# The last rotary score product on 128 rows of the array in place of 64

## The chip, the core and the metric

The kernel runs on one core of one Trainium2 chip. The metric is the device time of one execution in microseconds (us). Three runs of the kernel before gave 1396.41, 1398.60 and 1401.24 us; their median is 1398.6 us. TensorE (PE in the rows) multiplies matrices; VectorE (DVE), ScalarE (ACT) and GpSimd (POOL) do the rest, and nearly all transfers are issued from the queue of SyncE (SP).

## The reference, cut to what matters

One layer of a hybrid block on 1024 tokens: an input projection, a gated delta rule, latent attention with a rotary part, an output projection with a norm, a gated MLP, and a last norm. The change lies in the attention. Its four heads share one rotary key of 64 features, and its scores are

```python
s = jnp.einsum("bqhd,bkhd->bhqk", qn, k_nope) + jnp.einsum("bqhd,bkd->bhqk", qr, k_rope)
q_chunk = (blk * Q_BLOCK + jnp.arange(Q_BLOCK)) // CHUNK
allowed = key_chunk[None, :] <= q_chunk[:, None]
s = jnp.where(allowed, s.astype(jnp.float32) * scale, -jnp.inf)
pr = jax.nn.softmax(s, axis=-1).astype(v.dtype)
return jnp.einsum("bhqk,bkhd->bqhd", pr, v)
```

with 128 features without rotation (qn, k_nope) and 64 with it (qr, k_rope), and queries in 8 blocks of 128.

## The kernel before

**Numbers in two parts.** TensorE multiplies operands of type float32r. To keep float32 accuracy a value is split into a high part, rounded to float32r, and a low part, the rest. A product of two such values is then three products: high by high, low by high and high by low.

**A block of scores.** `score(h, qb)` (line 1146) makes the scores of head h and query block qb: 128 queries against the (qb + 1) * 128 keys that they may see, in one or two pieces b of at most 512 keys. Each piece is a sum of five matmuls into one bank: three for the features without rotation (`qnh` by `knh`, `qnh` by `knl`, `qnl` by `knh`), and two for the rotary ones. For these a tile `q_rot[h][hf]` has the high parts of the 64 rotary query features in rows 0 to 63 and the low parts in rows 64 to 127, and a tile `k_hh[b]` has the high parts of the keys twice, in the lower and the upper 64 rows. So the fourth matmul, `q_rot` by `k_hh` on 128 rows, does high by high and low by high at once. The fifth does high by low: it takes rows 0 to 63 of `q_rot` against `k_ll[b]`, the low parts of the keys, a tile of 64 rows. There are 32 blocks and 48 pieces, so 48 matmuls of each of the five kinds.

**What uses the scores.** `softmax` puts the mask into the block (a memset on VectorE), takes the maximum on VectorE, the exponential on ScalarE, and scales on VectorE. `transposed` turns the probabilities on TensorE (tiles `pt`), splits them (`pth` on ScalarE, `ptl` on VectorE), and `attended` multiplies them with the values (tiles `ov`). In round n the loop at line 1263 does the scores of pair n of query blocks between the transposes and products of pair n - 2. Scores lie in two banks of kind A, so a block waits for the exponential of the block before the last. In the rounds of the last head VectorE and ScalarE also split the weights of the output projection (tiles `wo`).

**Where the rotary keys come from.** `split_keys` (line 965) runs for both halves hf of the keys, while the last input projections (tiles `cq`) are on TensorE: ScalarE casts the high part, GpSimd subtracts for the low part, and SyncE's queue copies the high part to the upper rows of `k_hh`. The rotary queries are rotated later on VectorE and GpSimd (`rotate_queries`), written to `rot_d` in device memory and read back as `q_rot`.

**What sets the order.** A planner of coroutines with rough times decides at build time in which order the instructions are written: `wait(tile)` gives the time until a tile is ready by the planner's own clock, and a coroutine that yields goes on that much later. Every engine then runs its instructions in the written order, and SyncE's queue issues its transfers in order too, each one behind the waits of those ahead.

Of the kernel before, what the change touches and what calls it, by code (L numbers as in the profile page):

```python
# [17 lines left out]
P = 128  # L18
# [52 lines left out]
def hybrid_block_kernel(  # L71
# [22 lines left out]
    def SR(name, shape=None):  # L94
        return S(name, shape, F32R)
# [8 lines left out]
    # Coroutines yield the time until they go on; the clock is the tensor engine's. Rough times of the  # L104
    # instructions tell when a tile is ready.
# [32 lines left out]
    def settle(*aps):  # L138
        """Lets the others go on until the tiles are ready."""
        while events and wait(*aps) > 0.0 and events[0][0] < clock[0] + wait(*aps):  # L140
            hop()
# [5 lines left out]
    def book(engine, cost, delay, outs, ins):  # L147
        """The time at which an instruction ends."""
        near = delay if engine == "pe" else 0.0
        at = max([clock[0], busy.get(engine, 0.0)]  # L150
                 + [ready.get(k, 0.0) - (near if writer.get(k) is engine else 0.0) for k in outs + ins])
        busy[engine] = at + cost
        for k in outs:
            ready[k], writer[k] = at + cost + delay, engine
        for k in outs + ins:
            used[k] = max(used.get(k, 0.0), at + cost + delay)
        return at + cost

    class Engine:
        """An engine whose instructions are booked, and go out in the order in which they are written if pinned."""  # L160
# [49 lines left out]
    def room(*tags):  # L210
        """The time until a bank of each kind can be had."""
        return max(0.0, max(used.get(banks[t][0], 0.0) for t in tags) - clock[0])
# [30 lines left out]
    def split_w(src, shape, name, sub=None):  # L243
        """DMA a weight block and split it into two float32r parts whose sum is the block."""
# [6 lines left out]
    def prepare(w, src, shape, name, tags=("raw", "whi", "wlo")):  # L251
        """split_w, spread over the time it takes."""
# [9 lines left out]
    def mm3(outs, nk, w_hi, w_lo, r_hi, r_lo, order=((0,), (1,), (2,))):  # L262
        """outs[i] = sum_k w(k)^T r(k, i): three float32r products per block."""
# [8 lines left out]
    def rsqrt(y, v, n, e=None):  # L272
        """y = v^-0.5 on [P, n]: a bit-level first guess and Newton steps."""
        e = e or dve
        a = T(f"rs_a{n}", n)
# [7 lines left out]
    def inverse_root(y, h, e=None, between=()):  # L283
        """y = (2 h)^-0.5 on [P, 1], as rsqrt; other work fills the pauses."""
# [25 lines left out]
    # The first tokens come by halves of the features, so that the first products start early.  # L310
# [70 lines left out]
    # The tensor engine's clock doubles after some microseconds of work.  # L381
# [141 lines left out]
    def conv_half(f, y, ps, hf, then):  # L523
        """One half of a causal convolution of width 4 and its SiLU."""
# [14 lines left out]
    # Keys stay as they are: with r = 1 / |k|, the normed rule is that of k with the strength beta r^2  # L539
    # and the values v / r, so that only per-token factors change.  # L540
# [31 lines left out]
    def decays():  # L572
        """exp(G_i - G_j) of the running sums of the log decays, 0 above the diagonal."""
# [89 lines left out]
    def inverse(j):  # L663
        """The L of two chunks becomes ((I + L)^-1)^T, by 32 -> 64 -> 128 block elimination."""
# [55 lines left out]
    def chunk(t):  # L720
        """What chunk t needs besides the state: the attention inside it, its query norms and values."""
# [23 lines left out]
    def step(t):  # L745
        """The new values of chunk t and the state after it."""
# [34 lines left out]
    def chunk_out(t, qc, et, vn, state):  # L781
        """The outputs of chunk t, normed, gated and feature-major."""
# [85 lines left out]
    # The queries stay without the factor of their norm, which the softmax applies with its scale.  # L868
# [19 lines left out]
    def token_factors(name, rs, n):  # L888
        """1 / the root mean square over the n features, [token, block]."""
# [60 lines left out]
    def rotate_keys():  # L950
        """In place."""
# [13 lines left out]
    def split_keys():  # L965
        for hf in range(2):
            hh, ll = SR(f"k_hh{hf}"), SR(f"k_ll{hf}", [64, 512])
            split(hh[0:64], ll, krr[hf], pool)
            yield wait(hh)
            sync.dma_start(out=f32(hh[64:128]), in_=f32(hh[0:64]))  # L970
            k_hh.append(hh)
            k_ll.append(ll)
            yield 2.0
# [172 lines left out]
    def score(h, qb):  # L1146
        """Starts the probabilities of a query block, [query, key]."""
# [5 lines left out]
        for b in range((nk + 511) // 512):  # L1153
# [6 lines left out]
            mm(o_, q_rot[h][hf][0:64, qs], k_ll[b][:, 0:n], start=False)  # L1160
# [5 lines left out]
    def transposed(h, qq, j2):  # L1166
        """The probabilities of two query blocks for two key blocks, [key, query], split; 0 above the diagonal."""
# [29 lines left out]
    def attend(h, qq):  # L1197
        """Yields where a block of scores fits in."""
# [15 lines left out]
    def split_wide(name, src, tag):  # L1214
        """A [P, 2, 512] block as two pairs of float32r parts."""
# [19 lines left out]
    # The delta rule's part of the output projection of the first tokens fills in where attention leaves room.  # L1235
# [74 lines left out]
    def row_factors(st, n, e=None):  # L1310
        """The means of the rows and what gives 1 / deviation."""
# [9 lines left out]
    def layer_norm(r, g, b, e=None, last=None):  # L1321
        """r [P, 2, 512], over its whole rows, in place."""
# [19 lines left out]
    def transpose_h(hf, k2):  # L1342
        """Two of the blocks of h^T."""
# [12 lines left out]
    # The blocks of h^T (features of the lower and upper half, tokens of the first and second) and their sums  # L1356
    # T1 = B12 - B11, T2 = B22 - T1, T3 = B22 - B12, -T4 = B21 - T2, as pairs of parts.
# [3 lines left out]
    def add_up(hf, k, x):  # L1361
        """What block k of h^T, x, gives to the sums."""
# [90 lines left out]
    # The gates, by halves q of the columns, in Winograd's form of Strassen's product as explained below: A = w^T in  # L1453
    # blocks of column halves and halves of the inner sum, B = h^T.
# [51 lines left out]
    def gate_rows(q, i, j, c):  # L1506
        """Column quarter 2 q + i of the rows of half j gets its gated embedding; c: the sums with the bias."""
# [40 lines left out]
    def embed_rows(n, t):  # L1548
        """The projected embeddings of a row block."""
# [32 lines left out]
    g_d = [tc.dram_tile([P, 1024], F32, name=f"g{f}_d") for f in range(NFT)]  # L1582

    # u^T = w^T h^T for a feature of the gate and its partner, by Winograd's form of Strassen's product: with
    # A = w^T in 2 x 2 blocks (gate and partner, halves of the inner sum), S1 = A21 + A22, S2 = S1 - A11,
    # S3 = A11 - A21, S4 = A12 - S2 and P1 = A11 B11, P2 = A12 B21, P3 = S4 B22, P4 = A22 T4, P5 = S1 T1,
    # P6 = S2 T2, P7 = S3 T3 it is C11 = P1 + P2, C12 = P1 + P6 + P5 + P3, C21 = P1 + P6 + P7 - P4,
    # C22 = P1 + P6 + P7 + P5. Sums of products stay in PSUM where they can.
    ffn = [{} for _ in range(NFT)]

    def operand(f, i):
        """The left operand of product i of feature block f."""
# [41 lines left out]
    def conv(f, n, y, src):  # L1634
        """y = the convolution of src, a half of the tokens."""
# [5 lines left out]
    def conv_edge(f, n, y, before):  # L1641
        """What the tokens before it give to the second half."""
# [48 lines left out]
    # out = g w for pairs of feature blocks in the same form: A = g in blocks of token halves and the two features,  # L1691
    # B = w in blocks of the two features and column halves.
# [41 lines left out]
    def prepare_down(n):  # L1734
        """The operands of a step, and sums for later ones; gives out the vector engine's work."""
# [35 lines left out]
    # The features left over, in the plain way: gT[f][half] and wd[f][half] as pairs of parts.  # L1771
# [17 lines left out]
    def down_last(gT, wd, g, b):  # L1789
        """The last features; every row block is normed and goes out as soon as it is complete."""  # L1790
# [8 lines left out]
        def sum_factors(r, sums, e):  # L1799
            """row_factors from the sums of the halves of the rows."""  # L1800
# [160 lines left out]
```

## Time and profile before

| | |
|---|---|
| median of three runs | 1398.6 us |
| lowest, highest | 1396.41, 1401.24 us |
| span of the profiled execution | 1395.9 us |
| busy in the span: PE, DVE, ACT, POOL | 1354.1, 985.0, 626.6, 189.5 us |
| attention's stretch | from about 402 to 545 us of the span |
| mean granted clock of TensorE | 0.988 of full speed |

The span runs from the first to the last instruction of one profiled execution; the profile gives no other time of that execution. The median of the runs is 2.7 us above it. A matmul's duration in the rows includes its way through the array and overlaps with the next one's; what a matmul takes from the stream is the distance between its start and the next start.

### The profile page before, as it was taken

The page shows a single profiled execution, that of the slowest core. Times are in us where ns is not written, and L with a number is a line of the kernel's source. Part 1 is how long each engine was busy: PE and PEld are TensorE (multiplying, and loading weights), DVE is VectorE, ACT ScalarE, POOL GpSimd, SP SyncE. Part 2 cuts the span into 40 slices and gives each one's busy share as a digit, 9 for nine tenths or more (in the row PEclk, how much of TensorE's full clock was granted, in tenths as well). Part 3 has the DMA queues.
Part 4 walks back from the last instruction along what each step waited for, and adds up shares of the span by engine and source line. Part 5 has one row for each costly group of instructions (what it writes and reads, how often), then busy time and mean ns, then how long its engine had stood idle before and what let it go on. Part 6 is the DMA issues. An engine that isn't in the chain of part 4 may idle for free.

```text
span 1395.9 us, 19833 instructions
## 1 busy us (share of the span) xinstructions
PE 1354.1 (97%) x7185; PEld 1127.2 (81%) x7185; DVE 985.0 (71%) x1781; ACT 626.6 (45%) x1213; POOL 189.5 (14%) x418
## 2 busy tenths in 40 slices
PE   9999997999989999999999999999999999999995
PEld 6788885888867877888998888888888888888884
DVE  3646233365366675776989888888888887998857
ACT  3444223555434454135535555555555555444511
POOL 0231540034430000221000000000000000000026
PEclk9999998999999999999999999999999999999998
DMA  7035434434431224335552222222222239505112
GB/s 215 30 114 163 122 111 99 142 100 147 119 112 42 84 65 142 91 108 166 190 182 65 91 91 88 78 83 69 91 91 91 76 127 386 173 9 205 53 41 102
DMA packets 180929, 158.93 MB, mean 114 GB/s; under 512 B 26106, under 2 KB 140640, under 8 KB 180832
## 3 DMA queue, kind: packets, MB, share of 16 engines
q1 hardware_dynamic: 180624, 157.41, 36.3%
q8 instruction: 56, 0.92, 0.3%
q14 instruction: 41, 0.34, 0.1%
q10 hardware_dynamic: 144, 0.26, 0.1%
q0 software_dynamic: 64, 0.00, 0.0%
HBM read 117.53 MB, written 39.85 MB: 113 GB/s over the span
## 4 chain that ended last, share of the span: by engine, by line
PE 65%; DVE 4%; POOL 2%; ACT 2%; issue 2%; DMA 1%; SPq 0%; DVEq 0%; ACTq 0%; POOLq 0%
PE ffX L198 17%; PE ffZ L198 9%; PE dX L198 7%; PE dP L198 5%; PE ffY L198 4%; PE s L198 4%; PE mixp L198 4%; PE gX L198 3%; PE ov L198 2%; PE cq L198 2%; PE gY0P L198 1%; PE gY1P L198 1%; POOL rs_u L169 1%; PE pt L201 1%; DVE h L169 1%
## 5 line engine op out<-in xcount | busy, mean ns | idle before, releaser
L169 POOL TENSOR_SCALAR ln_v<-ln_ss 128x1 f32<-128x1 f32 x7 | 9.0, 1285 | 710.6 <-ACT sink L169 710.1
L198 PE MATMUL dX<-dP,dP 128*128 128x512 f32 x432 | 99.5, 389 | 0.0
L198 PEld LDWEIGHTS dX<-dP,dP 128*128 128x128 f32 x432 | 81.0, 188 | 17.1 <-DVE h L169 0.2
L169 DVE SCALAR_TENSOR_TENSOR gate<-c,vec,gate 128x511 f32<-128x511 f32 (+1 forms) x132 | 69.9, 571 | 11.4 <-ACT gate L169 10.6
L198 PE MATMUL dP<-dP,dP 128*128 128x512 f32 x324 | 75.4, 390 | 0.0
L198 PEld LDWEIGHTS dP<-dP,dP 128*128 128x128 f32 x324 | 60.6, 188 | 13.3 <-DVE h L169 0.9
L169 ACT CAST dP<-b 128x512 fp32r<-128x512 f32 x45 | 28.0, 622 | 59.6 <-issue 20.8
L169 ACT COPY c<-ffX 128x512 f32<-128x512 f32 x44 | 25.8, 586 | 38.9 <-PE ffX L198 38.9
L169 ACT ACTIVATE gate<-c,vec 128x512 f32<-128x512 f32 x44 | 35.9, 816 | 14.7 <-DVE c L169 12.6
L169 DVE SCALAR_TENSOR_TENSOR u<-ffX,vec,u 128x511 f32<-128x511 f32 (+1 forms) x88 | 40.2, 478 | 0.1
L169 ACT ACTIVATE p<-s,mx,q_f 128x128 f32<-128x128 f32 (+7 forms) x32 | 26.7, 835 | 28.6 <-DVE mx L169 26.7
L169 DVE SCALAR_TENSOR_TENSOR u<-c,vec,u 128x511 f32<-128x511 f32 (+1 forms) x44 | 33.0, 751 | 7.3 <-ACT u L169 6.6
L169 DVE TENSOR_TENSOR dP<-b,dP 128x512 fp32r<-128x512 f32 x45 | 31.1, 691 | 8.5 <-ACT dP L169 7.0
L169 ACT ACTIVATE gate<-gate 128x512 f32<-128x512 f32 x44 | 27.6, 627 | 12.2 <-DVE gate L169 12.2
L198 PE MATMUL ov<-pth,v 128*128 128x256 f32 x160 | 33.0, 299 | 0.1
L169 DVE TENSOR_TENSOR ptl<-pt,pth 128x512 fp32r<-128x512 f32 (+1 forms) x40 | 24.8, 633 | 11.1 <-ACT pth L169 10.6
L169 DVE TENSOR_TENSOR dP<-a,dP 128x512 fp32r<-128x512 f32 x45 | 31.0, 689 | 0.0
L169 DVE TENSOR_TENSOR u<-u,gate 128x512 f32<-128x512 f32 x44 | 30.1, 685 | 0.0
L169 ACT CAST dP<-a 128x512 fp32r<-128x512 f32 x45 | 27.7, 616 | 5.1 <-issue 2.2
L169 DVE SCALAR_TENSOR_TENSOR kt<-k,vec,kt 128x512 f32<-128x512 f32 (+3 forms) x24 | 16.4, 742 | 19.0 <-ACT kt L169 19.0
L169 POOL TENSOR_TENSOR h<-h,b 128x1024 f32<-128x1024 f32 x8 | 19.3, 2415 | 76.4 <-DVE h L169 75.1
L198 PEld LDWEIGHTS ov<-pth,v 128*128 128x128 f32 x160 | 24.8, 189 | 4.4 <-issue 1.8
(1373 smaller groups left out, 4181.1 us busy)
## 6 DMA issues: line engine op xcount, KB each, us to landing
wup<-in_ffn_w_up_dram SPq DMA_DIRECT2D x88, 256.0 KB
b<-in_ffn_w_down_dram SPq DMA_DIRECT2D x54, 256.0 KB
a<-g_d SPq DMA_DIRECT2D x45, 256.0 KB
g_d<-u SPq DMA_DIRECT2D x44, 256.0 KB
wgP_raw<-in_ple_w_gate_dram SPq DMA_DIRECT2D x16, 512.0 KB
wo_raw<-in_w_out_dram SPq DMA_DIRECT2D x8, 512.0 KB
xres<-in_x_dram SPq DMA_DIRECT2D x8, 512.0 KB
pp_d<-pp SPq DMA_DIRECT2D x16, 256.0 KB
```

The costliest lines, as they stand in the source:

```text
L169: ins = f(*a, **k)
L198: on_pe(nc.tensor.matmul(o, a, b, start=start, stop=stop, **k_), max((k - 1.0) * a.shape[-1] / 1900.0, n * k / 2370.0), o, a, b)
L201: on_pe(nc.tensor.transpose(o, a, i), 0.107, o, a)
```

## The change

The tiles `k_ll` get 128 rows. Their lower 64 rows are computed as before, and a new transfer on SyncE's queue copies them to the upper 64; for that `split_keys` also waits for `k_ll` in the planner's time. The fifth matmul takes all 128 rows of `q_rot`. It then also adds low by low. The diff also takes out comments, which are left out here.

```diff
     def split_keys():
         for hf in range(2):
-            hh, ll = SR(f"k_hh{hf}"), SR(f"k_ll{hf}", [64, 512])
-            split(hh[0:64], ll, krr[hf], pool)
+            hh, ll = SR(f"k_hh{hf}"), SR(f"k_ll{hf}")
+            split(hh[0:64], ll[0:64], krr[hf], pool)
             yield wait(hh)
             sync.dma_start(out=f32(hh[64:128]), in_=f32(hh[0:64]))
+            yield wait(ll)
+            sync.dma_start(out=f32(ll[64:128]), in_=f32(ll[0:64]))
             k_hh.append(hh)
             k_ll.append(ll)
             yield 2.0
...
             mm(o_, q_rot[h][hf][:, qs], k_hh[b][:, 0:n], start=False, stop=False)
-            mm(o_, q_rot[h][hf][0:64, qs], k_ll[b][:, 0:n], start=False)
+            mm(o_, q_rot[h][hf][:, qs], k_ll[b][:, 0:n], start=False)
             go()
```

On TensorE, VectorE and GpSimd the order of the instructions is the same. It differs on SyncE's queue and on ScalarE, in the last stretch of the input projections. On SyncE's queue, where the rotary keys are copied and weights for the attention are fetched (`wqr`, `wqn`, `wkn`), it is before

```order
L169 DMA wqr_raw<-in_mla_w_q_up_dram 128x4x32 x6
L169 DMA k_hh_3379<-k_hh_3379 64x512
L169 DMA k_hh_3410<-k_hh_3410 64x512
L169 DMA mix_d<-zc_3346 512x1x128
L169 DMA wqn_raw<-in_mla_w_q_up_dram 128x3x128
```

and now

```order
L169 DMA wqr_raw<-in_mla_w_q_up_dram 128x4x32 x6
L169 DMA k_hh_3379<-k_hh_3379 64x512
L169 DMA k_ll_3380<-k_ll_3380 64x512
L169 DMA mix_d<-zc_3346 512x1x128
L169 DMA k_hh_3439<-k_hh_3439 64x512
L169 DMA k_ll_3440<-k_ll_3440 64x512
L169 DMA wqn_raw<-in_mla_w_q_up_dram 128x3x128
```

Two copies are new, and the second half's copy of `k_hh` stands behind the write of `mix_d`; the fetch of `wqn` stands behind all of them.

On ScalarE at the same place, where the second half of the keys (`krr_181`) is cast between the compressed queries (`cqh`, their squares `cqq`), it is before

```order
L169 CAST k_hh_3379<-krr_180 64x512
L169 CAST k_hh_3410<-krr_181 64x512
L169 ACTIVATE cqh_0_3427<-cq_3132,vec_176 128x512
L169 ACTIVATE cqh_1_3428<-cq_3132,vec_176 128x512
L169 ACTIVATE cqq_0_3435<-cq_3132 128x512
L169 ACTIVATE cqq_1_3438<-cq_3132 128x512
L169 CAST wqr_hi<-wqr_raw 128x384
```

and now

```order
L169 CAST k_hh_3379<-krr_180 64x512
L169 ACTIVATE cqh_0_3423<-cq_3132,vec_176 128x512
L169 ACTIVATE cqh_1_3424<-cq_3132,vec_176 128x512
L169 ACTIVATE cqq_0_3431<-cq_3132 128x512
L169 ACTIVATE cqq_1_3434<-cq_3132 128x512
L169 CAST k_hh_3439<-krr_181 64x512
L169 CAST wqr_hi<-wqr_raw 128x384
```

The cast of the second half has moved behind four instructions. A little further on ScalarE two copies of the query product (`qr`) have moved ahead of the second cast of `wqn`, before

```order
L169 CAST wkn_hi<-wkn_raw 128x256
L169 CAST wqn_hi<-wqn_raw 128x384
L169 COPY qr_3570<-qr_3509 128x512
L169 COPY qr_3571<-qr_3509 128x512
L169 COPY qr_3595<-qr_3574 128x512
```

and now

```order
L169 CAST wkn_hi<-wkn_raw 128x256
L169 COPY qr_3568<-qr_3511 128x512
L169 COPY qr_3569<-qr_3511 128x512
L169 CAST wqn_hi<-wqn_raw 128x384
L169 COPY qr_3597<-qr_3572 128x512
```

so the copies no longer stand behind that cast.

## Rows read from the trace of the kernel before

**Rows 1.** The page: busy us, share of the span and instructions of each engine.

```profile
PE 1354.1 (97%) x7185; PEld 1127.2 (81%) x7185; DVE 985.0 (71%) x1781; ACT 626.6 (45%) x1213; POOL 189.5 (14%) x418
```

**Rows 2.** Busy time by stretch of attention: stretch, length, engines, clock, DMA share.

```profile
402.00:430.00 28.00, 24.20 (x106) 16.80 (x105) 14.88 (x43) 9.93 (x22) 0.00 (x0) 0.94 0.18 63
430.00:520.00 90.00, 89.13 (x523) 71.33 (x522) 61.19 (x153) 46.41 (x102) 5.17 (x22) 1.00 0.21 66
520.00:540.00 20.00, 18.66 (x94) 12.95 (x93) 16.14 (x38) 13.75 (x29) 0.82 (x4) 1.00 0.47 151
...
510.80:521.80 11.00, 10.88 (x69) 8.73 (x68) 10.61 (x27) 9.00 (x22) 0.42 (x2) 1.00 0.41 122
```

**Rows 3.** Timeline of TensorE's matmuls: start us, duration us, what (x2: two).

```profile
462.95 0.50 PE L198 MATMUL s<-kn1h,qn1h 128*128 128x512 f32 x1
463.29 0.40 PE L198 MATMUL s<-kn1l,qn1h 128*128 128x512 f32 x1
463.53 0.39 PE L198 MATMUL s<-kn1h,qn1l 128*128 128x512 f32 x1
463.75 0.40 PE L198 MATMUL s<-k_hh,q_rot 128*128 128x512 f32 x1
464.08 0.50 PE L198 MATMUL s<-k_ll,q_rot 64*128 64x512 f32 x1
464.51 0.51 PE L198 MATMUL ov<-pth,v 128*128 128x256 f32 x2
```

**Rows 4.** Timeline around 432 us: first TensorE's matmuls.

```profile
432.19 0.28 PE L198 MATMUL s<-k_hh,q_rot 128*128 128x256 f32 x1
432.40 0.38 PE L198 MATMUL s<-k_ll,q_rot 64*128 64x256 f32 x1
```

**Rows 5.** The same stretch: TensorE's weight loads.

```profile
432.07 0.19 PEld L198 LDWEIGHTS s<-k_hh,q_rot 128*128 128x128 f32 x1
432.40 0.18 PEld L198 LDWEIGHTS s<-k_ll,q_rot 64*128 64x128 f32 x1
432.78 0.19 PEld L198 LDWEIGHTS s<-kn1h,qn1h 128*128 128x128 f32 x1 [0.20 <-ACT p L169]
```

**Rows 6.** The tile s: both rotary matmuls, durations ns min/median/max, and their forms.

```profile
L198 PE MATMUL s<-k_hh,q_rot x48: 278/387/416, 406.5 to 532.5; 128*128 128x512 f32 x24, 128*128 128x256 f32 x16, 128*128 128x384 f32 x8
L198 PE MATMUL s<-k_ll,q_rot x48: 379/492/579, 406.8 to 532.8; 64*128 64x512 f32 x24, 64*128 64x256 f32 x16, 64*128 64x384 f32 x8
```

**Rows 7.** Timeline of TensorE: the starts that waited, [us idle before, releaser].

```profile
406.54 0.36 PE L198 MATMUL s<-k_hh,q_rot 128*128 128x256 f32 x1 [2.56 <-DMA q_rot<-rot_d]
416.95 0.50 PE L198 MATMUL s<-kn0h,qn0h 128*128 128x512 f32 x1 [1.23 <-ACT p L169]
434.61 0.39 PE L198 MATMUL ov<-ptl,v 128*128 128x256 f32 x1 [0.35 <-DVE ptl L169]
526.98 0.50 PE L198 MATMUL s<-kn3h,qn3h 128*128 128x512 f32 x1 [0.68 <-ACT p L169]
```

**Rows 8.** Timeline of VectorE in the last head: where it waited for scores.

```profile
522.22 0.11 DVE L169 MEMSET s<- 64x64 f32 x1 [0.41 <-PE s L198]
524.81 0.11 DVE L169 MEMSET s<- 64x64 f32 x1 [0.77 <-PE s L198]
533.43 0.11 DVE L169 MEMSET s<- 64x64 f32 x1 [1.10 <-PE s L198]
```

**Rows 9.** Timelines of ScalarE and GpSimd where the keys are split and weights cast.

```profile
362.22 2.54 POOL L169 TENSOR_TENSOR k_ll<-krr,k_hh 64x512 fp32r<-64x512 f32 x2
369.93 0.52 ACT L169 CAST wqr_hi<-wqr_raw 128x384 fp32r<-128x384 f32 x1
376.79 0.54 ACT L169 CAST wqn_hi<-wqn_raw 128x384 fp32r<-128x384 f32 x1
381.33 0.51 ACT L169 CAST wqn_hi<-wqn_raw 128x384 fp32r<-128x384 f32 x1 [3.70 <-DMA wqn_raw<-in_mla_w_q_up_dram]
```

**Rows 10.** Timeline of SyncE's queue: issues of transfers in the same stretch.

```profile
369.19 0.62 SPq L169 DMA_DIRECT2D wqn_raw<-in_mla_w_q_up_dram  x1
```

## The prediction

> **What bounds the kernel now.** I read the page first: TensorE is busy for 1354.1 of 1395.9 us [rows 1], so only what shortens its stream, or lengthens a wait in it, can count. Next I read the busy times by stretch. Between 430 and 520 us TensorE is busy for 89.13 of 90 us, while VectorE has 61.19 and ScalarE 46.41 [rows 2]; the scores lie in a stretch that TensorE bounds. It is less clear before 430, where TensorE misses 3.8 us, and after 520, where it misses 1.34 us and VectorE is at 16.14 of 20 [rows 2].
>
> Then the timeline, and in it the distances between starts. One piece of scores of 512 keys begins at 462.95 and the next work begins at 464.51: 1.56 us for five matmuls [rows 3]. The ordinary distance is 463.29 to 463.53 and 463.53 to 463.75, 0.23 on average [rows 3], so five would take 1.15 to 1.18 us. The excess of 0.38 to 0.41 us has three places: 463.75 to 464.08 ahead of the fifth product (0.33, so 0.10 too long), 464.08 to 464.51 behind it (0.43, 0.20 too long), and the first matmul after the one before, 462.95 to 463.29 (0.34, 0.11 too long) [rows 3]. The loads show why. For the fourth product the load starts at 432.07, ahead of its matmul at 432.19; for the fifth, load and matmul both start at 432.40 [rows 4, 5]. So the load of 64 rows does not begin under the product before it, and the next load of 128 rows does not begin under the 64-row product either. The load itself is no longer than others: 0.18 against 0.19 us [rows 5].
>
> What else could be special about the fifth product? It uses the same tile `q_rot` as the fourth, but the second product of a piece also uses the stationary tile of the first (qn1h) and has the ordinary distance behind it [rows 3]. It also ends a sum, which these rows can't tell apart; that is left to the second rival. What remains is its 64 rows.
>
> **The change, part by part.** *The fifth product.* There are 48, with 512, 256 and 384 keys [rows 6], and the excess is a load's, so it doesn't depend on the number of keys. I worked out the same three distances for the other pieces, the first at 406.8 and the last at 532.8 [rows 6]: where no wait falls in them the excess is 0.37 to 0.40 us, 0.386 on average. With 128 rows the fifth product is what the fourth is, whose load lies under the product before it [rows 4, 5]. So 48 x 0.386 = 18.5 us leave TensorE's stream. This is the upper end. The nearest lower one is the difference of the durations, 492 against 387 ns in the median [rows 6]: 48 x 0.105 = 5.0 us, what would be left if the late loads stayed and only the product itself became ordinary. I take the upper value, since the distances between starts are what the stream loses, and no row gives another cause.
>
> *What of it reaches the end.* Where TensorE waits for others anyway, a shorter stream makes the wait longer. I go through the waits [rows 7].
> - 406.54, for `q_rot`: it lies ahead of the first fifth product; nothing lost.
> - 416.95, 1.23 us for an exponential: it needs the maximum on VectorE, which stands behind the mask of the next block, which needs that block's scores. So the wait moves with the scores, and only the part behind the last fifth product (0.20 + 0.11) is lost: 0.3 us.
> - 434.61 and the load at 432.78 that waited 0.20 for an exponential [rows 5, 7]: here the second head begins with its two smallest blocks while the first head's last softmax is still under way. That softmax sets the pace, and the two fifth products in between give nothing: 2 x 0.386 = 0.8 us lost.
> - 526.98, 0.68 us for an exponential: as at 416.95, behind the scores; 0.3 us lost.
>
> In the last head VectorE also splits output weights and is busy for 10.61 of 11.00 us between 510.80 and 521.80 [rows 2]. It has an order of its own and can't be hurried. From there to 524.8 the blocks 2 to 5 of that head have 1 + 1 + 2 + 2 = 6 fifth products, 2.3 us. VectorE's own gaps there are 0.39 in the full stretch, 0.41 and 0.77 [rows 2, 8], together 1.6: 0.7 us lost. Blocks 6 and 7 have 4 more, 1.5 us, against a gap of 1.10 [rows 8] and smaller ones: 0.3 lost. The losses come to 0.3 + 0.8 + 0.3 + 0.7 + 0.3 = 2.4 us, so 18.5 - 2.4 = 16.1. I take off 0.4 more for waits too small for these rows to show: **15.7 us**.
>
> *The two new copies.* Each is a transfer of 128 KB like that of `k_hh`, and ends over 30 us before the first fifth product at 406.8; nothing.
>
> *The moved steps.* The cast of the second keys moves on ScalarE to 369.9, just ahead of `wqr` [rows 9]; GpSimd then needs 1.27 us, half of 2.54, for the low part [rows 9], so the last new copy is issued near 372. SyncE's queue holds the fetch of `wqn` behind it: issue at some 372.4 and not 369.19 [rows 10], 3.2 us later. Its cast comes at 376.79 [rows 9], so it has 4.4 us; the later fetch of `wqn` on which ScalarE waited until 381.33 comes behind other waits and keeps its time. The wait of 3.70 us there no longer holds up the two copies of `qr`, since these now go first; they can start some 0.5 us earlier, which helps nobody, because GpSimd and VectorE behind them wait for others. I take zero. The bounds are a gain of 0.5 and a loss of 3.2 us, if the whole delay of the fetch came through.
>
> **Rivals.**
> *VectorE and ScalarE take over (1389.4).* With TensorE's 18 us gone VectorE's 14.88 + 61.19 + 16.14 = 92 us of these 138 [rows 2] are a share of 77%, and its order is fixed. If each of the 16 smaller pieces (blocks 0 to 3 of each head) and the 12 pieces of the last head, less the 4 in both, gave nothing, 24 x 0.386 = 9.3 us would be left. For it: the waits of rows 7 are all softmax. Against: from 430 to 520 TensorE waited for less than 1 us, and the large blocks leave VectorE gaps of over a microsecond.
>
> *The fifth product costs what it did (1398.6 down to 1393.6).* If the late load has to do with something other than the rows, the change gives 0, or at most the 5.0 us of the durations. Against it: among the rows shown only the fifth product, without waiting for anything, has load and start together. The Trainium skill, page "TensorE: Matmul & The Clock Gate", section "LDWEIGHTS (loading the stationary operand)", says that a load takes as long for 32 rows as for 128, only its columns count, and a table in that page's section "Why this matters for your kernels" that a product on 32 rows takes the time of one on 128. By that rule alone the sum would be zero; the load's own 0.18 and 0.19 us agree with it, but not the distances in rows 3, which that rule leaves out.
>
> *Slower: the queue holds up the queries' weights (1403).* The place is SyncE's queue at 370 to 372. If `wqn` lands later than its cast needs it (over 4.4 us late, 3.2 of which are accounted for, so from 1.2 us more), ScalarE's queue stops in front of the `qr` copies, the rotation and `q_rot` come later, and TensorE, already waiting 2.56 us there [rows 7], waits up to 3.2 us more; a longer wait would also lengthen the stretch of lower clock behind it (0.94 granted from 402 to 430 [rows 2]), an estimated 1 us. That makes 4.2 us. It ends above the time before only if the fifth products give less than 4.2 / 48 = 0.09 us each, so together with the rival above. Otherwise it takes 4.2 from the 15.7.
>
> **How the numbers follow.** Chances: the forecast 0.74, VectorE and ScalarE take over 0.13, the fifth product costs what it did 0.10, slower 0.03. The span would be 1395.9 - 15.7 = 1380.2; the median of the runs lies 2.7 above that span, so the time is 1398.6 - 15.7 = 1382.9 us. The low end is the full 18.5 us and 1.1 for the spread of the runs, 1379.0; the high end takes in the rival of the softmax chain, 1389.4, and rounds to 1390. A measurement of this kernel can tell about 0.3%, 4.2 us, from no change. Faster by more: the forecast, the softmax rival and a third of the next one, 0.74 + 0.13 + 0.03 = 0.90; within it 0.08; slower 0.02.
>
> **What would show it.** The fifth product must stand as 128*128, with its load starting ahead of it, and 0.23 us behind the fourth for 512 keys; a piece must take 1.15 to 1.18 us. The weight loads' idle time ahead of `k_ll` must go. The stretch from 402 to 540 must be shorter by some 15 us, and the rest as long as before. The waits at the second head's start and VectorE's gaps in the last head must change as told: the first longer by some 0.8, the second gone. The prediction is wrong if the load still starts with its matmul, if TensorE's waits for softmax grow by more than 4 us, or if the first product with `q_rot`, at 406.54 before, moves by more than 1 us.

## The result and the profile after

The changed kernel took 1380.07 us in the median of four runs (1378.43 to 1380.62), beside 1397.74 us, the median of four runs of the kernel before in the same comparison. The ratio is 0.9861, with a 95% interval from 0.9844 to 0.9878. On the 1398.6 us of the first section that is 1379.2 us (1376.8 to 1381.5), so 19.4 us less (17.1 to 21.8); the forecast was 15.7 less. On the 1397.74 us it is 1378.3 us. The two medians alone give a smaller gain, 17.7 us. The sign and the mechanism came as foretold, but the gain by the ratio is larger than the 18.5 us that the prediction set as the most: the time lies at the low end of the range (1379.0) or just under it, and 1382.9 us lies above the interval.

The page, as in [rows 1]: TensorE is busy for 19.9 us less, the number of instructions of these engines is the same, and no other engine changed by more than 3 us.

```profile
PE 1334.2 (97%) x7185; PEld 1126.2 (82%) x7185; DVE 987.7 (72%) x1781; ACT 626.8 (46%) x1213; POOL 188.9 (14%) x418
```

The tile `k_ll` in both views, first the weight loads and then the matmuls (durations in ns, min/median/max, first and last start in us, forms), to be held against [rows 6]:

```profile
L198 PEld LDWEIGHTS s<-k_ll,q_rot x48: 187/188/192, 403.6 to 512.7; 128*128 128x128 f32 x48
L198 PE MATMUL s<-k_ll,q_rot x48: 279/384/395, 403.7 to 512.9; 128*128 128x512 f32 x24, 128*128 128x256 f32 x16, 128*128 128x384 f32 x8
```

The median of the fifth product fell from 492 to 384 ns, close to the 387 of the fourth [rows 6]. The same piece of scores as in [rows 3], matmuls first (start us, duration us), then the weight loads around the fifth product:

```profile
451.97 0.40 PE L198 MATMUL s<-kn1h,qn1h 128*128 128x512 f32 x1
452.21 0.39 PE L198 MATMUL s<-kn1l,qn1h 128*128 128x512 f32 x1
452.44 0.40 PE L198 MATMUL s<-kn1h,qn1l 128*128 128x512 f32 x1
452.67 0.39 PE L198 MATMUL s<-k_hh,q_rot 128*128 128x512 f32 x1
452.90 0.39 PE L198 MATMUL s<-k_ll,q_rot 128*128 128x512 f32 x1
453.13 0.40 PE L198 MATMUL ov<-pth,v 128*128 128x256 f32 x2
```

```profile
452.67 0.19 PEld L198 LDWEIGHTS s<-k_ll,q_rot 128*128 128x128 f32 x1
452.90 0.41 PEld L198 LDWEIGHTS ov<-pth,v 128*128 128x128 f32 x2
```

The piece takes 453.13 - 451.97 = 1.16 us and not 1.56. The load for the fifth product starts at 452.67, with the fourth product, 0.23 ahead of its own matmul; the next load starts at 452.90, with the fifth product. All three late places of [rows 3] are ordinary distances now. In the piece of [rows 3] itself, these were the loads for the first product, right behind a fifth one, and for the fifth:

```profile
462.95 0.19 PEld L198 LDWEIGHTS s<-kn1h,qn1h 128*128 128x128 f32 x1 [0.25 <-issue]
464.08 0.18 PEld L198 LDWEIGHTS s<-k_ll,q_rot 64*128 64x128 f32 x1 [0.36 <-issue]
```

Both loads start with their own matmul, and the engine waited for nothing that the profile shows ("issue"). The load at 432.78 of [rows 5], from which the prediction read that the load behind a 64-row product is late, had also waited for an exponential; the one at 462.95 had not.

The waits that answer to [rows 7], from the timeline of TensorE ([us idle before, releaser]):

```profile
403.55 0.36 PE L198 MATMUL s<-k_hh,q_rot 128*128 128x256 f32 x1 [2.46 <-DMA q_rot<-rot_d]
412.54 0.50 PE L198 MATMUL s<-kn0h,qn0h 128*128 128x512 f32 x1 [1.23 <-ACT p L169]
425.28 0.39 PE L198 MATMUL s<-kn1h,qn1h 128*128 128x256 f32 x1 [0.24 <-ACT p L169]
426.93 0.39 PE L198 MATMUL ov<-ptl,v 128*128 128x256 f32 x1 [0.55 <-DVE ptl L169]
508.36 0.50 PE L198 MATMUL s<-kn3h,qn3h 128*128 128x512 f32 x1 [0.69 <-ACT p L169]
```

All starts above are some 3 us earlier from the beginning, since the first product with `q_rot` moved from 406.54 to 403.55. In `again`, the changed kernel once more, it stands at 406.52, so the 3 us are not the change's (below, "What varies by itself"), and I measure attention from that product to the first product of the output projection (`mixp<-wo00h,mixg_hi`): 538.48 - 406.54 = 131.94 us before and 518.41 - 403.55 = 114.86 after. That is **17.08 us** of the 48 x 0.386 = 18.53 that the prediction set as the most.

The stretches that answer to [rows 2] (the first at the same times of the trace, so 8 to 20 us later in the work), full attention and the saturated part of the last head (length, busy time of PE, PEld, DVE, ACT and POOL, granted clock, DMA share, GB/s):

```profile
430.00:520.00 90.00, 88.29 (x568) 79.22 (x567) 71.22 (x171) 55.92 (x120) 5.22 (x24) 1.00 0.31 98
494.70:505.50 10.80, 10.80 (x72) 9.79 (x73) 10.55 (x27) 8.98 (x21) 0.62 (x3) 1.00 0.47 144
```

VectorE's 61.19 us of 90 have become 71.22, and in the last head it is busy for all but 0.25 us; TensorE still misses only 1.7 us of the 90.

### The profile page after: what moved, and what is told of

The parts are those of the page before. It is cut to its first block, busy times and chain, and to the rows that moved or that the text cites. A ratio compares the mean times of both kernels' runs of the same rounds, so it can differ in the third digit from the quotient of the medians.

```text
span 1376.4 us, 19840 instructions
## 1 busy us (share of the span) xinstructions
PE 1334.2 (97%) x7185; PEld 1126.2 (82%) x7185; DVE 987.7 (72%) x1781; ACT 626.8 (46%) x1213; POOL 188.9 (14%) x418
## 4 chain that ended last, share of the span: by engine, by line
PE 64%; DVE 5%; POOL 2%; ACT 2%; issue 2%; DMA 1%; SPq 0%; DVEq 0%; ACTq 0%; POOLq 0%
PE ffX L198 17%; PE ffZ L198 9%; PE dX L198 7%; PE dP L198 5%; PE ffY L198 4%; PE mixp L198 4%; PE gX L198 3%; PE s L198 3%; PE ov L198 2%; PE cq L198 2%; PE gY0P L198 1%; PE gY1P L198 1%; POOL rs_u L169 1%; PE pt L201 1%; DVE h L169 1%
## 5 line engine op out<-in xcount | busy, mean ns | idle before, releaser
L198 PEld LDWEIGHTS dX<-dP,dP 128*128 128x128 f32 x432 | 81.0, 188 | 17.1 <-DVE h L169 0.2
L169 ACT ACTIVATE u<-ffX,vec 128x512 f32<-128x512 f32 x22 | 17.2, 780 | 22.9 <-PE ffX L198 22.9
```

The lines of the kernel that those rows point to most:

```text
L169: ins = f(*a, **k)
L198: on_pe(nc.tensor.matmul(o, a, b, start=start, stop=stop, **k_), max((k - 1.0) * a.shape[-1] / 1900.0, n * k / 2370.0), o, a, b)
```

## The experiments

What they had to tell apart is, first, whether the 64 rows of the fifth product are the cause, or the new copies, the moved steps or the added values; second, whether the price hangs on the product or on the change between 64 and 128 rows; third, how much the last head loses.

**The changed kernel and the kernel before once more** (`again`, `before_again`).

> The changed kernel once more, to size the gain and to tell the part outside attention. Theory A (64 rows make the loads late, 48 x 0.386 us leave TensorE's stream, about 1.5 lost in waits): the way from the first q_rot product to the first mixp product is 17 us shorter than before, 114.9 against 131.9 us, in this profile too; the time is 17 to 18 us under that before. Theory B (the change also shortens the stretch of half clock between 217 and 235 us, by which the first trace was 2.9 us ahead when attention began): the inverse stage ends some 3 us early in this profile too, and the time is 19 to 20 us under that before.

> The kernel before once more, for the stretch from 217 to 235 us, which lay 2.9 us apart in the first two traces. Theory A (the length of the stretch at half clock differs from execution to execution): the way from the first inverse product to the first z product's successors, ending with the first ckv product, takes anything between the 22.8 us of the changed and the 25.6 us of the kernel before. Theory B (the change shortens it): 25.6 us again.

`again`: 1380.42 us, ratio 0.987 (0.9855 to 0.9886), attention 114.93 us. `before_again`, a single run: 1399.89 us, attention 132.05 us. Attention repeats to 0.1 us in both, so it is the measure for what follows. The stage of the inverses took 23.42 and 23.25 us: both kernels come out between the 22.8 and 25.6 of the first two traces, so its length varies with the execution, which is theory A of `before_again`.

**The copies without the wide product** (`copy_only`). Against the changed kernel:

```diff
-            mm(o_, q_rot[h][hf][:, qs], k_ll[b][:, 0:n], start=False)
+            mm(o_, q_rot[h][hf][0:64, qs], k_ll[b][0:64, 0:n], start=False)
```

> The whole change but one thing: the fifth product stays on rows 0 to 63 of both tiles. The low parts are laid down twice, with the new transfers and the moved steps. Theory A: the late loads stay, the time is that before within 0.1% (1396 to 1400 us), and the fifth product's load starts with its matmul. Rival C (the copies, the moved cast or the new positions of the tiles bring part of the gain): 3 us or more faster than before.

1398.6 us, ratio 1.0005 (0.9996 to 1.0013). The matmuls of `k_ll`, in the same view as above, are those of [rows 6] again:

```profile
L198 PE MATMUL s<-k_ll,q_rot x48: 379/492/579, 406.8 to 534.4; 64*128 64x512 f32 x24, 64*128 64x256 f32 x16, 64*128 64x384 f32 x8
```

So the two copies and the steps that moved on SyncE's queue and on ScalarE cost and give nothing that can be measured. Attention took 133.49 us, 1.5 more than before, all of it in the first head, where the clock was lower for longer (0.50 granted from 410 to 412 us, and 0.81 in the kernel before); from the second head on it is 106.72 against 106.73 us.

**Zeros in the upper rows** (`zero_rows`). The kernel before in its order, with the fifth product on 128 rows whose upper 64 rows of keys GpSimd sets to zero; low by low is then left out:

```diff
-            hh, ll = SR(f"k_hh{hf}"), SR(f"k_ll{hf}", [64, 512])
-            split(hh[0:64], ll, krr[hf], pool)
+            hh, ll = SR(f"k_hh{hf}"), SR(f"k_ll{hf}")
+            split(hh[0:64], ll[0:64], krr[hf], pool)
...
+            nc.gpsimd.memset(f32(ll[64:128]), 0.0)
...
-            mm(o_, q_rot[h][hf][0:64, qs], k_ll[b][:, 0:n], start=False)
+            mm(o_, q_rot[h][hf][:, qs], k_ll[b][:, 0:n], start=False)
```

> The fifth product on 128 rows, but the upper 64 rows of the low parts are zeros that GpSimd writes; so no new transfer, no wait in the planner, and the order of ScalarE and SyncE's queue is that before. The sum is what it was before the change. Theory A: all of the gain, as in the changed kernel within 1 us (17 to 18 us under the time before). Rival C: less than that by what the moved steps brought.

1381.38 us, ratio 0.9877 (0.9862 to 0.9893), attention 114.89 us: the gain comes without the copies and without the added term.

**Without the planner's wait** (`no_wait`). The changed kernel less the line `yield wait(ll)`; the transfer itself still waits for its tile.

> The changed kernel without the planner's wait for the low parts, so that the casts of the keys stand on ScalarE as before and the two new copies stand each behind that of the high parts. Theory A: the moved steps cost and bring nothing, so the changed kernel's time within 1 us. Rival (the moved steps cost part of the gain, or bring part of it): 1 to 3 us away from it.

1381.48 us, ratio 0.9874 (0.9852 to 0.9896), attention 114.88 us. The moved steps are worth nothing that can be measured in either direction.

**96 rows** (`rows96`). The changed kernel with the fifth product on rows 0 to 95, so that half of low by low is left out:

```diff
-            mm(o_, q_rot[h][hf][:, qs], k_ll[b][:, 0:n], start=False)
+            mm(o_, q_rot[h][hf][0:96, qs], k_ll[b][0:96, 0:n], start=False)
```

> The changed kernel with 96 rows in the fifth product in place of 128 (low by low is added for half of the features). Theory A1 (the array is set up for 64 or for 128 rows, 96 counts as 128, and only a change between the two makes loads late): the whole gain, 17 to 18 us. Rival A2 (any load of fewer than 128 rows is late, since it leaves part of the array as it was): no gain, 1396 to 1400 us.

1382.8 us, ratio 0.9889 (0.9872 to 0.9906), attention 115.06 us, 0.2 more than with 128. The weight loads of this kernel, and below them those of the kernel before:

```profile
L198 PEld LDWEIGHTS s<-k_ll,q_rot x48: 187/188/330, 407.3 to 516.5; 96*128 96x128 f32 x48
L198 PEld LDWEIGHTS s<-k_ll,q_rot x48: 182/183/285, 406.8 to 532.8; 64*128 64x128 f32 x48
```

The load has the 188 ns of a full one, where that of 64 rows had 183, and the distances are the ordinary ones. So it is not that some rows of the array are left unused; 96 rows stand with 128. What fewer than 64 rows or the upper 64 rows alone would do, no run shows.

**Both rotary products on 64 rows** (`both64`). The kernel before, with the fourth product on 64 rows too (low by high is left out), so twice the number of 64-row products at the same number of changes:

```diff
-            mm(o_, q_rot[h][hf][:, qs], k_hh[b][:, 0:n], start=False, stop=False)
+            mm(o_, q_rot[h][hf][0:64, qs], k_hh[b][0:64, 0:n], start=False, stop=False)
```

> The kernel before with the fourth product on 64 rows too, so that two 64-row products follow each other (the product of the queries' low parts with the keys' high parts is left out). Theory A1 (only a change between 64 and 128 rows makes loads late): as many changes as before, so the time before within 2 us, and the distance from the fourth to the fifth product is the ordinary 0.23 us for 512 keys. Rival A2 (every 64-row load is late, whatever stands ahead of it): 48 x 0.1 to 0.3 us more, 1403 to 1413 us.

1402.94 us, ratio 1.0028 (1.0017 to 1.0039). From the second head's first product to the output projection it takes 106.72 us, where the kernel before takes 106.73: 36 more products on 64 rows cost nothing there. The two rotary matmuls and the weight loads of a piece show it ([us idle before, releaser]):

```profile
464.13 0.49 PE L198 MATMUL s<-k_hh,q_rot 64*128 64x512 f32 x1
464.46 0.39 PE L198 MATMUL s<-k_ll,q_rot 64*128 64x512 f32 x1
```

```profile
464.12 0.18 PEld L198 LDWEIGHTS s<-k_hh,q_rot 64*128 64x128 f32 x1 [0.37 <-issue]
464.23 0.19 PEld L198 LDWEIGHTS s<-k_ll,q_rot 64*128 64x128 f32 x1
464.79 0.19 PEld L198 LDWEIGHTS s<-kn1h,qn1h 128*128 128x128 f32 x1 [0.37 <-issue]
```

Now the first of the two 64-row loads is the late one; the second is pulled ahead under the first product; the 128-row load behind them is late again. The distance from the fourth to the fifth product is 0.33 us, not the 0.23 expected; `paired64` below shows why. What I had also not expected are 4.4 us in the first head, 29.59 us against 25.21 from the first product with `q_rot` to the second head. They go with a second stretch of half clock. TensorE's busy time by stretch (length, busy, instructions, granted clock, DMA share, GB/s), first of `both64`, then of the kernel before:

```profile
416.00:418.00 2.00, 0.84 (x3) 1.00 0.26 98
418.00:420.00 2.00, 2.00 (x7) 0.63 0.20 76
420.00:424.00 4.00, 4.00 (x10) 0.50 0.00 1
424.00:428.00 4.00, 4.00 (x18) 0.50 0.05 16
428.00:430.00 2.00, 2.00 (x8) 0.81 0.10 33
```

```profile
416.00:420.00 4.00, 3.05 (x12) 1.00 0.21 79
420.00:424.00 4.00, 4.00 (x24) 1.00 0.00 0
```

In both, TensorE had just waited 1.23 us for an exponential (at 417.16 and 416.95); only with both rotary products on 64 rows did the clock fall to half, 1.2 GHz, some microseconds behind it. The timed runs go with it: nine of the ten of `both64` had a mean clock of 0.983 or 0.984, and the one with 0.987, what most runs of the kernel before had, took 1399.4 us. Why the one falls and the other doesn't, these runs do not settle.

**Fifth products in pairs** (`paired64`). The kernel before, with 64-row products in the same number, but in the 16 blocks of two pieces the two fifth products stand back to back:

```diff
             mm(o_, q_rot[h][hf][:, qs], k_hh[b][:, 0:n], start=False, stop=False)
+            go()
+        for b in range((nk + 511) // 512):
+            n = max(256, min(512, nk - 512 * b))
+            o_ = ps[:, b * 512:b * 512 + n]
             mm(o_, q_rot[h][hf][0:64, qs], k_ll[b][:, 0:n], start=False)
```

> The kernel before, with the fifth products still on 64 rows, but in a block of two pieces the two fifth products stand back to back at the end of the block, behind both fourth products. There are 16 such blocks, so the array changes between 128 and 64 rows 32 times there and back and not 48 times. Theory (the price is one per change there and back, some 0.386 us): 16 x 0.386 = 6.2 us less, of which some 0.5 goes into waits of the last head; 5.7 us faster, 1393, attention from the first product with q_rot to the first of the output projection 126.3 us and not 132.0; the second of two fifth products in a row is 0.23 us behind the first with its load ahead. Rival (each 64-row product pays for itself): no change, attention 132.0 us. A third: the second product pays half, 3 us.

1392.04 us, ratio 0.9947 (0.9935 to 0.996), attention 125.61 us: 6.3 us less, against 16 x 0.386 = 6.2 and 5.7 expected: the 0.5 that was taken off for waits of the last head was not lost. Matmuls and then loads at the end of a block (x2: two instructions):

```profile
460.69 0.39 PE L198 MATMUL s<-kn1h,qn1l 128*128 128x512 f32 x1
460.91 0.39 PE L198 MATMUL s<-k_hh,q_rot 128*128 128x512 f32 x1
461.23 0.49 PE L198 MATMUL s<-k_ll,q_rot 64*128 64x512 f32 x1
461.57 0.39 PE L198 MATMUL s<-k_ll,q_rot 64*128 64x512 f32 x1
461.89 0.50 PE L198 MATMUL ov<-pth,v 128*128 128x256 f32 x2
```

```profile
461.23 0.18 PEld L198 LDWEIGHTS s<-k_ll,q_rot 64*128 64x128 f32 x1 [0.35 <-issue]
461.34 0.19 PEld L198 LDWEIGHTS s<-k_ll,q_rot 64*128 64x128 f32 x1
461.89 0.30 PEld L198 LDWEIGHTS ov<-pth,v 128*128 128x128 f32 x2 [0.36 <-issue]
```

The pair takes 461.89 - 461.23 = 0.66 us, 0.20 more than two ordinary distances, what the one product of [rows 3] took too much behind it. Here the 0.20 stands in two places. The load of the second product starts ahead of its matmul, at 461.34, but the distance between the two is 0.34 and not the 0.23 expected: 0.11 too long, as behind the first 128-row product after a change, 462.95 to 463.29 in [rows 3]. The distance ahead of the change back is 0.32, 0.09 too long, as the one ahead of the change to 64 rows, 460.91 to 461.23. So each change of rows, in either direction, costs about 0.1 us ahead of its first product and 0.1 behind it; with a single 64-row product the two in the middle fall together. The price is one per change from 128 to 64 rows and back, not one per product. The Trainium skill, page "TensorEngine Tiling (Array Packing)", section "Key Properties", says that a change of the tiling mode, not of the tile alone, drains TensorE. If a product on 64 rows counts as another mode, the traces of `both64` and `paired64` agree with it and put a size to it here: 0.386 us there and back.

**Wide only in the last head** (`head3_only`).

```diff
+            r = P if h == 3 else 64
-            mm(o_, q_rot[h][hf][:, qs], k_ll[b][:, 0:n], start=False)
+            mm(o_, q_rot[h][hf][0:r, qs], k_ll[b][0:r, 0:n], start=False)
```

> The changed kernel, but only the last head's fifth products take 128 rows; those of the first three heads take 64 as before. Theory: there are 12 pieces in the last head, so 12 x 0.386 = 4.6 us is the most; the prediction took 0.7 + 0.3 off for VectorE there and 0.3 for the exponential at its start, which leaves 3.3; the traces of before and after give 31.55 - 27.57 = 3.98 us from the last head's first product to the output projection's first. If that head's gain does not depend on the others it is 4.0 again, 1394.8 us, and the first three heads stand as before. Rival (the last head can only gain because softmax came into it with a lead): 3 us or less.

1395.01 us, ratio 0.997 (0.9958 to 0.9982), 4.2 us by the ratio. From the last head's first product to the output projection it takes 27.60 us, against 31.55 before and 27.57 in the changed kernel. The last head gains 3.96 to 3.98 of its 12 x 0.386 = 4.63 us, whatever the heads before it do.

**Another tile for the rotated queries** (`two_rot`, `two_rot_2`, beside `after_2`). The wait of 2.46 us for `q_rot` is still there after the change. The read of the first half of the first head's `q_rot` stands on SyncE's queue behind the writes of both halves, since both go through one tile `rot_d`. With a tile for each half it stands ahead of the second half's writes:

```diff
-    rot_d = tc.dram_tile([2, 2, 2, P, 512], F32, name="rot_d")
+    rot_d = [tc.dram_tile([2, 2, P, 512], F32, name=f"rot_d{hf}") for hf in range(2)]
...
-        yield wait(rot_d)
+        if hf:
+            yield wait(rot_d[hf])
```

> The changed kernel, and the rotated queries go through two tiles in device memory, one for each half of the queries, so that the first half of the first head's q_rot is fetched ahead of the second half's writes and not behind them. It aims at the wait of 2.5 us in front of the first product with q_rot and at the stretch of half clock behind it. Theory: the wait goes (2.5 us) and the half clock with it (up to 1 us more), 2 to 3.5 us faster than the changed kernel, 1377 to 1378. Rival: the fetch on the in-order queue makes the second half's writes later, and block 4, the first that needs the second half, waits instead; then 0 to 1 us.

> The changed kernel once more, beside the one with two tiles for the rotated queries on the same chip. Attention from the first product with q_rot to the first of the output projection 114.9 us as in the two executions before; the stage of the inverses between 22.8 and 25.6 us, whichever half-clock stretch it meets; 1380 us.

> The kernel with two tiles for the rotated queries once more. If the wait for q_rot (2.46 us before, 0.25 in the first execution of this kernel) and the half-clock stretch behind it (114.9 against 113.3 us of attention) are gone for good, it takes 2.2 + 1.5 = 3.7 us less than the changed kernel, less what the inverse stage varies; if the half clock only came elsewhere, 2 us or less.

1377.59 us, ratio 0.9853 (0.984 to 0.9867), and on the chip of the second comparison 1376.81 us, ratio 0.9848 (0.9834 to 0.9863), beside 1379.08 us, ratio 0.9869 (0.9853 to 0.9885), for the changed kernel. The wait in the first of the two, and the clock of the stretch behind it, of `two_rot` and then of the changed kernel (all engines: PE, PEld, DVE, ACT, POOL, then clock, DMA share, GB/s):

```profile
404.15 0.36 PE L198 MATMUL s<-k_hh,q_rot 128*128 128x256 f32 x1 [0.25 <-DMA q_rot<-rot_d]
```

```profile
404.00:408.00 4.00, 3.85 (x21) 3.39 (x22) 2.80 (x12) 1.73 (x6) 0.21 (x1) 1.00 0.16 53
```

```profile
404.00:408.00 4.00, 4.00 (x15) 3.29 (x14) 1.97 (x11) 1.68 (x5) 0.00 (x0) 0.57 0.26 100
```

The wait shrinks from 2.46 to 0.25 us, and in the second comparison from 2.02 to 0.51. Behind it TensorE stays at the full 2.4 GHz, where in the changed kernel it was granted 0.57 of that on average, and attention takes 113.33 and 113.31 us against 114.86 to 114.93. In the timed runs the medians of the second comparison differ by 2.3 us, where the 2.2 + 1.5 us of the expectation would be 3.7; the two intervals overlap, so the traces show the gain better than the times do. Both medians of this version lie below the three of the changed kernel (1379.08 to 1380.42 us).

## Why the prediction was off

**What held.** The cause was the 64 rows among 128: the three distances, their sum of 0.386 us, the 48 times, and the load as the place were all as worked out. The moved steps were worth zero (`copy_only`, `no_wait`). The rival by which the fifth product costs what it did is refuted. For it stood the Trainium skill, page "TensorE: Matmul & The Clock Gate", section "Why this matters for your kernels", which gives a single product on 32 rows the time of one on 128. No run here has such a product by itself. On 64 rows the duration of a load agrees with it (183 ns, and 188 on 128); the distances in a stream of 128-row products do not. VectorE and ScalarE did not take over. The queue of SyncE did not hold up the queries' weights: `wqn` was issued 0.5 us behind the last new copy at 369.15, in this trace, which is some 3 us early there, and its cast did not wait.

```profile
369.15 0.46 SPq L169 DMA_DIRECT2D k_ll<-k_ll  x1
369.66 0.58 SPq L169 DMA_DIRECT2D wqn_raw<-in_mla_w_q_up_dram  x1
373.82 0.54 ACT L169 CAST wqn_hi<-wqn_raw 128x384 fp32r<-128x384 f32 x1
```

**By the prediction's own sign.** It called itself wrong if the first product with `q_rot` moved by more than 1 us, and that product moved by 2.99. But it also stands at 407.18 in `before_again`, at 406.52 in `again` and at 403.28 in `after_2`: the sign tells executions apart, not the two kernels. What failed in the prediction are the sizes of two terms, the losses in waits and the 1.1 us for the spread of the runs.

**The first mis-sized term: the losses in waits.** The prediction took off 0.3 + 0.8 + 0.3 + 0.7 + 0.3, and 0.4 for waits not shown, 2.8 us. The trace gives 18.53 - 17.08 = 1.45. Landmark by landmark, with the start before and after:

| stretch | fifth products, at most | gained | lost | predicted lost |
|---|---|---|---|---|
| first `q_rot` product to the wait at 416.95 / 412.54 | 4: 1.54 | 1.42 | 0.12 | 0.3 |
| second head's start: 431.75 to 434.61 / 424.20 to 426.93 | 2: 0.77 | 0.13 | 0.64 | 0.8 |
| last head's first product to 526.98 / 508.36 | 8: 3.09 | 2.53 | 0.56 | 0.3 + 0.7 |
| from there to the output projection | 4: 1.54 | 1.45 | 0.09 | 0.3 |
| all the rest | 30: 11.58 | 11.55 | 0.03 | 0.4 |

The second head's start went as told: 0.24 us ahead of the second block, now on the matmul itself, and 0.35 grown to 0.55 ahead of `ov`. In the stretches of the table's last row TensorE had no long wait, and their 30 products gave 11.55 / 30 = 0.385 us each, so the price itself was sized right. The largest miss is the last head, 0.65 lost in place of 1.3. There I let VectorE give back only the gaps in which it waited for scores [rows 8] and the 0.39 of one chosen stretch [rows 2]. All three gaps of [rows 8] are gone, as told. But VectorE also waited for ScalarE's `pth`, which comes from TensorE's transposes and so moves with them. These gaps stood just outside what I had looked at. The first two rows are of before, the third of after ([us idle before, releaser]):

```profile
510.73 0.56 DVE L169 TENSOR_TENSOR ptl<-pt,pth 128x384 fp32r<-128x384 f32 x1 [0.73 <-ACT pth L169]
527.43 0.69 DVE L169 TENSOR_TENSOR ptl<-pt,pth 128x512 fp32r<-128x512 f32 x1 [0.80 <-ACT pth L169]
```

```profile
508.82 0.69 DVE L169 TENSOR_TENSOR ptl<-pt,pth 128x512 fp32r<-128x512 f32 x1 [0.38 <-ACT pth L169]
```

The 0.73 us is gone and the 0.80 has shrunk to 0.38, so VectorE had 1.15 us more slack than my sum gave it, about twice the 0.65 that the sum was wrong by there. That these pauses gave the 0.65 is read from the rows, not tried on its own. `head3_only` shows that the last head gains its 3.96 us by itself, so it did not need a lead from the heads before.

**The second: the spread of the runs.** The two profiled executions differ by 19.5 us and attention by 17.08. The other 2.4 are not the change's. They come from the stage of the inverses (next section): 25.56 us in the profiled execution of before, 22.79 in that of after, 2.77 less, but 23.25 in `before_again` and 23.42 in `again`. The rest of the span is 0.4 us longer. The other comparisons of equal or equivalent kernels gave ratios of 0.987, 0.9877, 0.9874 and 0.9869, 17.2 to 18.3 us. So the 19.4 us of the first comparison is the upper end of what such comparisons give, and the low end of the range, the full 18.5 and 1.1 for the spread, had hardly room for it. The range's low end was set as if all losses could be zero, but the spread of the runs was taken too small: four runs of before alone spread over 4.8 us, and three of them, with the same lowest and highest, were known beforehand.

## What varies by itself

In two places TensorE runs at half clock for a stretch whose length differs between executions of one kernel. TensorE's clock from 225 to 235 us, before and after (granted clock behind the busy times), where the order of work is the same in both:

```profile
225.00:230.00 5.00, 5.00 (x58) 0.50 0.43 110
230.00:235.00 5.00, 5.00 (x27) 0.67 0.00 0
```

```profile
225.00:230.00 5.00, 5.00 (x64) 0.81 0.38 104
230.00:235.00 5.00, 5.00 (x74) 1.00 0.00 0
```

TensorE is busy throughout and has 53 more matmuls in the second. The stage took 22.8 to 25.6 us over the 14 profiled executions, with both ends among equal orders of work. A second place, in the trace of `after_2` and of `two_rot_2`, which are equal up to there (all engines, then the clock):

```profile
292.00:296.00 4.00, 4.00 (x36) 3.99 (x36) 2.58 (x7) 0.48 (x3) 2.55 (x13) 1.00 0.81 228
```

```profile
292.00:296.00 4.00, 4.00 (x26) 4.00 (x26) 1.01 (x3) 0.00 (x0) 2.10 (x11) 0.67 0.68 191
```

The matmul shortly ahead of it had waited 0.24 us in both. In the one the clock stays, in the other it falls, and 1.6 us are gone. Of the 14 executions 10 have it; of the three of the changed kernel, `again` has it, the other two don't. Whether the pause brings it on, no run shows. It is one reason why `two_rot_2`, with 1.6 us less of attention, has a span only 1.2 us shorter than `after_2` (1374.6 and 1375.8). A third stretch of half clock, the one behind the wait for `q_rot`, hardly differs between executions of one kernel: from there to the second head it is 25.21 and 25.32 us in the two executions of before, 20.65 to 20.68 in the three of the changed kernel.

## What to carry to other kernels

Look at distances between starts, not at durations: a product on 64 rows among products on 128 showed a load of the usual length, and yet cost 0.386 us, with neither its own load nor the next one begun under the product before. Fill the rows if there is something to fill them with (zeros do), or put such products side by side, so that the array changes less often. And when a shorter stream is set against a busy engine's slack, count all its gaps, also those in which it waits for a third engine that itself follows the stream; here that is read from the rows and not tried.

## What was not expected of the hardware

- 96 rows have the distances of 128; 64 rows don't (`rows96`, `before`).
- A second 64-row product right behind the first is free of the price; each change of rows costs about 0.2 us, half ahead of its first product and half behind it (`both64`, `paired64`).
- Leaving out half of a product's rows made the kernel slower, by 4 us, through a half-clock stretch in the first head alone (`both64`).
- A fall of the clock, some microseconds behind a pause of 0.24 us, comes in some executions of the same program and not in others (`again`, and not `after_2`).
